# Heads of grouped attention as steps between weight blocks, in a decoder trunk on one core

## The chip, the cores and the metric

One NeuronCore of a Trainium2 chip runs one launch that computes the whole trunk in fp32. The metric is device time in microseconds (us), a median over several runs. TensorE (PE; its weight loads are PEld), VectorE (DVE), ScalarE (ACT), GpSimd (POOL) and SyncE (SP) each work through a queue of their own in order and wait for one another by semaphores.

## The reference

Four layers run over 256 tokens of width 2048. Layers 0 and 3 are latent attention, layer 1 is sparse attention (an indexer picks the keys of each query), layer 2 is sliding-window attention with sinks. Every layer also has four memory heads and a gate:

```
h = rmsnorm(x)
q, k, v, (indexer), mq, gate = split(h @ w_in)
self heads  : softmax(q k^T * scale + bias + mask) v     # 32 heads in 4 groups of 8
memory heads: softmax(mq mk^T * scale) mv                # 4 heads of 256
x = x + ((self ++ memory) * silu(gate)) @ w_out
```

Layers 1 and 2 share one table of relative-position biases, a row for each head. In layer 1 the bias is added to the mask of the selection first; in layer 2 a sink joins the softmax.

## The kernel before, in words

**Weights.** Products keep nearly fp32 precision by being split in two: a value is a high part plus a low part, and three matmuls (high by high, high by low, low by high) make one product. Weights stream from memory once. `stage` issues the load of a block (two tiles of 128x512, 512 KB) on SP's queue into one of five buffers `wr`. `parts_of` turns a tile into `wh` (ScalarE copies it with rounding, L60) and `wl` (VectorE, `wr` minus `wh`, L69); either has three buffers:

```
wh = wp.tile([P, 512], F32R, name="wh", tag="wh", bufs=3)
wl = wp.tile([P, 512], F32R, name="wl", tag="wl", bufs=3)
```

`rows_by` (L265 to L267) multiplies the activations of two blocks of 128 tokens, one PSUM accumulator each, with a block of 512 weight columns, one k tile after the other; `columns_by` (L285, L289) does the same with tokens along the columns, for the gate. PSUM has four accumulators, so two column blocks can be open at a time.

**Parts of a layer.** The branch of a layer has six parts: 4 and 5 are the memory heads in pairs, 0 to 3 the groups of eight self heads. They are taken in the order 4, 0, 1, 2, 3, 5. The output projection `w_out` of a part (four column blocks, four k tiles each, L1139 adds into `x`) is issued one part late: the code for part n+1 goes ahead of that for the projection of part n, which is `pending` until then.

**Grouped attention** (layers 1 and 2, class `Grouped`). `project(g)` multiplies out the queries of group g (`acc_q`), transposes them (`tr`) to `qS`, starts the load of the group's eight bias rows `bm` on POOL's queue and multiplies out the gate (`acc_g`, L483 and L484 its activation). `attend` runs the eight heads in the order 0, 2, 1, 3, 4, 6, 5, 7: scores (`sp`, L943, L946), bias (layer 2: L520, L522; layer 1: L955 first), exponentials (`e`, L527), their transposes (`ptp`, L502), split to `pT` for two heads at a time, and the product with the values (`o`, L972). After heads 1 and 3, and again after 5 and 7, `yt` is `o` times the gate (L978), and is split to the high and low halves of `y` for two of the four k tiles of `w_out`: heads 0 to 3 make k = 0, 1, heads 4 to 7 make k = 2, 3.

**Order.** `steps` is a list of generators: each call of `other_work`, one in every weight block, advances the first of them by two, and what they issue then stands between weight blocks in program order. In the program before they carry other side work (the selection of layer 1 among it), and `attend` issues all eight heads at one place. The order in each engine's queue is then set by the framework's scheduler, which may move an instruction ahead of others as far as dependencies and buffers allow; heads, transposes and weight tiles of neighbouring parts are mixed there already.

Of the kernel before, what the change touches and what calls it, by code (L numbers as in the profile page):

```python
# [8 lines left out]
F32 = mybir.dt.float32  # L9
# [6 lines left out]
P = 128  # L16
S = 256
# [9 lines left out]
N_TAB = 384  # L27
# [4 lines left out]
def kernel(ctx: ExitStack, tc: tile.TileContext, a: dict, out: bass.AP,  # L32
                             kinds=(0, 1, 2, 0)):
    nc = tc.nc
# [18 lines left out]
    def f32(ap):  # L53
        return ap.bitcast(F32)
# [174 lines left out]
    def other_work():  # L229
        for _ in range(2):  # L230
            if steps and next(steps[0], None) is None:
                steps.pop(0)

    def parts_of(wr, c0, n):
        wh = wp.tile([P, 512], F32R, name="wh", tag="wh", bufs=3)
# [238 lines left out]
    def gate(nm, w, c0):  # L474
        gT = act.tile([P, 4, S], F32, name="gT", tag="gT", bufs=2)
        for h in range(2):
            acc = columns_by(nm.at, 16, w, 0, (c0 + h * S, S), "g")
            for j in range(2):
                z = total(acc[j])
                hz = wk.tile([P, S], F32, name="hz", tag="z", bufs=3)  # L480
                nc.vector.tensor_mul(hz, z, nm.half)
                th = wk.tile([P, S], F32, name="th", tag="e", bufs=4)
                nc.scalar.activation(th, hz, AF.Tanh)  # L483
                nc.vector.scalar_tensor_tensor(gT[:, 2 * h + j, :], th, 1.0, hz, op0=OP.add, op1=OP.mult)  # L484
        return gT
# [65 lines left out]
    def memory_project(nm, i, w, mq0, g0, part, behind):  # L551
        kT, qT = [], []
        if part == 0:
            not_before(behind)
        v = [act.tile([P, 2, 512], F32R, name="mvr", tag="aux", bufs=AUX) for z in range(2)]
        pin = tc.keep_in_program_order if part == 0 else lambda inst: inst
        for z in range(2):
            pin(nc.gpsimd.dma_start(v[z], mv[i][part][:, z]))
        for h in range(2):
            k = act.tile([P, 2, 2, S], F32R, name="mkr", tag="pq", bufs=PQ)  # L560
            pin(nc.gpsimd.dma_start(k, mkT[i][2 * part + h]))
            kT.append(k)
            acc = columns_by(nm.at, 16, w, 0, (mq0 + part * 512 + h * 256, 256), "mq")
            q = act.tile([P, 2, 2, S], F32R, name="mqT", tag="pq", bufs=PQ)
            head_parts(q, acc)
            qT.append(q)
        return nm, kT, v, qT, gate(nm, w, g0 + 2048 + part * 512)
# [179 lines left out]
    class Grouped:  # L747
# [165 lines left out]
        def project(self, g):  # L913
            nm = self.nm
            acc = rows_by(nm.at, 16, self.w, 0, (g * 512, 512), "q")
            q = [act.tile([P, 4, S], F32R, name="qS", tag="pq", bufs=PQ) for z in range(2)]
            if self.sparse:
                for z in range(2):
                    rows_ = part_tile(F32)
                    for t in range(2):  # L920
                        copy_act(rows_[:, t * S:(t + 1) * S], acc[t][:, z * S:(z + 1) * S],
                                 scale=nm.col("eighth", t))
                    four_heads(q[z], [rows_[:, t * S:(t + 1) * S] for t in range(2)])
            else:
                for t in range(2):
                    self.stacked(lambda i0, i1: q[i0 // 4][:, :, t * P:(t + 1) * P], acc[t],
                                 nm.col("eighth", t), 8)
            bm = act.tile([P, 8, S], F32, name="bm", tag="big3")
            tab = tabs[0 if self.sparse else 1][g]
            nc.gpsimd.dma_start(bm, bass.AP(tensor=tab.tensor, offset=tab.offset + 127,  # L930
                                            ap=[[8 * N_TAB - 1, P], [N_TAB, 8], [1, S]]))
            return g, q, bm, gate(nm, self.w, self.g0 + g * 512)

        def attend(self, g, q, bm, gT):
            while steps:
                other_work()
            y = act.tile([P, 2, 4, S], F32R, name="y", tag="y", bufs=2)
            for h in (0, 2, 1, 3, 4, 6, 5, 7):
                def score(b):
                    sp = misc("sp")  # L940
                    qb = q[h // 4][:, h % 4, b * P:(b + 1) * P]
                    if b == 0:
                        nc.tensor.matmul(sp[:, :S], qb, self.k[:, g, :, :P], start=True, stop=True)  # L943
                    else:
                        for v in range(2):
                            nc.tensor.matmul(sp[:, :S], qb, self.k[:, g, v, :],  # L946
                                             start=v == 0, stop=v == 1)
                    return sp

                def bias(b, n):  # L950
                    bh = bm[:, h, S - n:]
                    if not self.sparse:
                        return bh
                    bs = wk.tile([P, S], F32, name="bs", tag="e", bufs=4)
                    nc.vector.tensor_add(bs[:, :n], bh, self.sel[:, b, :n])  # L955
                    return bs[:, :n]
                nsk = None if self.sparse else nsink[:, g * 8 + h:g * 8 + h + 1]
                tp = masked_softmax(score, bias, None, nsk)

                half, odd = h // 2 % 2, h % 2  # L960
                if half == 0:
                    pHL = [wk.tile([P, 3, 2, P], F32R, name="pT2", tag="pT", bufs=PT) for z in range(2)]
                split(pHL[0][:, :, half, :], pHL[1][:, :, half, :],
                      tp[:, :3 * P].rearrange("p (i c) -> p i c", i=3))
                if half == 0:
                    continue
                if not odd:
                    o = misc("o")
                v0 = g * P + (0 if odd else 64)
                for t in range(2):  # L970
                    for n_, (z, p_) in enumerate(((0, 0), (0, 1), (1, 0))):
                        nc.tensor.matmul(o[:, t * S:], self.vz[z][:, t, v0:v0 + P],  # L972
                                         pHL[p_][:, 2 * t:2 + t].rearrange("p i h c -> p (i h c)"),
                                         start=odd == t == n_ == 0, stop=odd == t == 1 and n_ == 2)
                if odd:
                    j = (h // 4) * 2
                    yt = tmp("yt")
                    nc.vector.tensor_mul(yt.rearrange("p (j b c) -> p j b c", j=2, b=2),  # L978
                                         o.rearrange("p (b j c) -> p j b c", b=2, j=2),
                                         gT[:, j:j + 2, :].rearrange("p j (b c) -> p j b c", b=2))  # L980
                    split(y[:, 0, j:j + 2, :], y[:, 1, j:j + 2, :], yt.rearrange("p (a b) -> p a b", a=2))
            return y


    def last_out(w, part, y):
# [140 lines left out]
    for i in range(depth):  # L1126
        kind = kinds[i]
        mixer = Latent(nm, i, kinds[:i].count(0)) if kind == 0 else Grouped(nm, i, kind == 1)
        mixer.first()
        if i == depth - 1:  # L1130
            steps.append(split_ahead(a["w_out"][i], 5))
        nxt = Norm(i + 1) if i + 1 < depth else None

        def w_out(part, y, last):
            for c in range(4):
                acc = rows_by([y], 4, a["w_out"][i], part * 4, (c * 512, 512), "wo")
                for t in range(2):
                    xs = x[t][:, c * 512:(c + 1) * 512]
                    nc.vector.tensor_add(xs, xs, acc[t])  # L1139
                if c == 0 and copies:  # L1140

                    not_before(xs[:, :1])
                    table_copies(*copies.pop(0))
                if last and nxt is not None:
                    nxt.chunk(c)

        pending = None
        order = [4, 0, 1, 2, 3, 5]
        for n_, part in enumerate(order):
            if part >= 4:  # L1150
                y = memory_attend(*memory_project(nm, i, mixer.w, mixer.mq0, mixer.g0, part - 4,
                                                  f32(mixer.k[:, 0] if kind else mixer.kr)[:, 0, :1]))
            else:
                y = mixer.attend(*mixer.project(part))
            if pending is not None:
                w_out(*pending, False)
            pending = (part, y)
        if nxt is None:
            last_out(a["w_out"][i], *pending)
        else:  # L1160
            w_out(*pending, True)
            nxt.finish()
            nm = nxt
# [62 lines left out]
```

## Time and profile before

| | us |
|---|---|
| median of 3 runs | 2582.67 |
| lowest and highest | 2582.4, 2584.72 |
| profiled execution | 2583.45 |
| its span, first to last instruction | 2581.7 |
| TensorE busy | 2569.7 (granted clock 0.999) |
| VectorE busy | 1885.5 |
| ScalarE busy | 1618.6 |
| POOL busy | 87.1 |

Busy time is the sum of an engine's instructions with overlaps counted once. Matmuls overlap, so the row of TensorE tells how seldom it stands still, not how fast it is. In the rows below, a line starts with the engine and line of the code (L265 is line 265), the output and its inputs by name, and the shape; `x` is a count, and what stands in brackets or after the last bar is idle time ahead of the instruction and who ended it. In rows by window, each engine has its busy time and its instructions, and then stand the granted clock, the share of the DMA engines and GB/s.

### The profile page before, as it was taken

How to read it: one execution, taken by the hardware profiler on the slowest of the kernel's cores; microseconds unless marked ns; L12 is line 12 of the kernel's file. 1: busy time of each engine (PE TensorE's matmuls, PEld its weight loads, DVE VectorE, ACT ScalarE, POOL GpSimd, SP SyncE). 2: the span in 40 equal slices, each digit the busy share in tenths (PEclk: the TensorE clock that was granted, in tenths of full speed). 3: DMA queues.
4: the chain of work that ended last, by engine and by line, in shares of the span. 5: the costliest groups of instructions: out<-in, count | busy, mean ns of one | idle time of the engine just before them, and what ended most of it. 6: DMA issues, size and time to landing. Idle time of an engine off the chain costs nothing. (4 is left out here: it accounts for less than half of the span.)

```text
span 2581.7 us, 41595 instructions
## 1 busy us (share of the span) xinstructions
PE 2569.7 (100%) x13986; PEld 2210.8 (86%) x13986; DVE 1885.5 (73%) x4139; ACT 1618.6 (63%) x3435; POOL 87.1 (3%) x159
## 2 busy tenths in 40 slices
PE   9999999999999999999999999999999999999998
PEld 7888898888888888888888888888888888888887
DVE  6666667677776686877778776777778767777676
ACT  6556556556656566667666666676666655665655
POOL 1000000000000010000000000000000000000000
PEclk9999999999999999999999999999999999999999
DMA  9888777666676667566556565555555877666664
GB/s 301 257 258 268 239 213 235 183 172 192 192 205 200 199 213 248 169 203 188 190 171 197 171 221 170 173 174 185 196 156 147 241 201 197 196 195 182 211 173 179
DMA packets 459416, 520.02 MB, mean 201 GB/s; under 512 B 69520, under 2 KB 353056, under 8 KB 457536
## 3 DMA queue, kind: packets, MB, share of 16 engines
q1 hardware_dynamic: 441744, 449.72, 58.1%
q0 software_dynamic: 16736, 66.65, 8.0%
q8 instruction: 110, 1.80, 0.3%
q14 instruction: 106, 0.87, 0.1%
q10 hardware_dynamic: 720, 0.98, 0.1%
HBM read 494.10 MB, written 35.75 MB: 205 GB/s over the span
## 5 line engine op out<-in xcount | busy, mean ns | idle before, releaser
L69 DVE TENSOR_TENSOR wl<-wr,wh 128x512 fp32r<-128x512 f32 (+2 forms) x1720 | 1159.9, 677 | 610.0 <-ACT wh L60 588.8
L60 ACT ACTIVATE wh<-wr 128x512 fp32r<-128x512 f32 (+2 forms) x1720 | 1065.3, 621 | 796.6 <-PE acc_g L285 176.9
L285 PE MATMUL acc_g<-xT,wh 128*128 128x512 f32 x1536 | 486.0, 396 | 0.0
L289 PEld LDWEIGHTS acc_g<-xT,wl 128*128 128x128 f32 x1536 | 284.6, 188 | 61.7
L289 PE MATMUL acc_g<-xT,wl 128*128 128x256 f32 x1536 | 307.9, 280 | 0.0
L266 PE MATMUL acc_wo<-wl,y 128*128 128x512 f32 x752 | 297.1, 395 | 0.2 <-DVE wl L69 0.2
L267 PE MATMUL acc_wo<-wh,y 128*128 128x512 f32 x752 | 292.0, 390 | 0.0
L285 PEld LDWEIGHTS acc_g<-xT,wh 128*128 128x128 f32 x1536 | 237.1, 189 | 2.7
L265 PE MATMUL acc_wo<-wh,y 128*128 128x512 f32 x752 | 234.5, 392 | 0.1
L266 PEld LDWEIGHTS acc_wo<-wl,y 128*128 128x128 f32 x752 | 141.3, 188 | 27.9 <-DVE wl L69 0.6
L267 PEld LDWEIGHTS acc_wo<-wh,y 128*128 128x128 f32 x752 | 141.3, 188 | 27.1
L265 PEld LDWEIGHTS acc_wo<-wh,y 128*128 128x128 f32 x752 | 139.1, 188 | 28.7 <-ACT y L60 1.0
L285 PE MATMUL acc_mq<-xT,wh 128*128 128x512 f32 x512 | 161.6, 396 | 0.0
L285 PE MATMUL acc_mk<-mT,wh 128*128 128x512 f32 x512 | 161.5, 396 | 0.1
L1139 DVE TENSOR_TENSOR x<-x,acc_wo 128x512 f32<-128x512 f32 x184 | 121.4, 681 | 3.7 <-PE acc_wo L267 3.6
L285 PE MATMUL acc_qn<-cT,wh 128*128 128x512 f32 x384 | 121.3, 397 | 0.0
L285 PE MATMUL acc_cq<-xT,wh 128*128 128x512 f32 x384 | 120.9, 396 | 0.0
L289 PEld LDWEIGHTS acc_mk<-mT,wl 128*128 128x128 f32 x512 | 96.1, 188 | 22.8 <-DVE wl L69 0.4
L289 PEld LDWEIGHTS acc_mq<-xT,wl 128*128 128x128 f32 x512 | 93.9, 188 | 20.1
L289 PE MATMUL acc_mq<-xT,wl 128*128 128x256 f32 x512 | 103.1, 281 | 0.0
L266 PE MATMUL acc_q<-wl,xT 128*128 128x512 f32 x256 | 101.2, 395 | 0.0
L289 PE MATMUL acc_mk<-mT,wl 128*128 128x256 f32 x512 | 101.1, 278 | 0.0
(328 smaller groups left out, 4326.2 us busy)
## 6 DMA issues: line engine op xcount, KB each, us to landing
wr<-in_w_out_dram SPq DMA_DIRECT2D x188, 512.0 KB, 3.7
wr<-in_w_in_a_dram SPq DMA_DIRECT2D x176, 512.0 KB, 4.5
wr<-in_w_mem_kv_dram SPq DMA_DIRECT2D x120, 512.0 KB, 4.6
wr<-in_w_in_b_dram SPq DMA_DIRECT2D x112, 512.0 KB, 3.4
wr<-in_w_in_c_dram SPq DMA_DIRECT2D x104, 512.0 KB, 3.5
wr<-in_w_uq_dram SPq DMA_DIRECT2D x192, 128.0 KB, 2.9
wr<-in_w_uq_dram SPq DMA_DIRECT2D x48, 256.0 KB, 3.8
tab<-flat POOLq DMA_DIRECT2D x8, 1536.0 KB, 9.7
```

Source lines behind the costliest of these rows:

```text
L60: inst = nc.scalar.activation(o, i, AF.Copy, scale=scale)
L69: nc.vector.tensor_sub(lo, src, f32(hi))
L265: nc.tensor.matmul(acc[t][:, :n], xh, wh[:, :n], start=first, stop=False)
L266: nc.tensor.matmul(acc[t][:, :n], xh, wl[:, :n], start=False, stop=False)
L267: nc.tensor.matmul(acc[t][:, :n], xl, wh[:, :n], start=False, stop=last)
L285: nc.tensor.matmul(acc[j], wh[:, o:o + P], q[:, :, kt % 4, :], start=kt == 0, stop=False)
L289: nc.tensor.matmul(acc[j][:, 0, :], wl[:, o:o + P], q[:, 0, kt % 4, :], start=False, stop=kt == kts - 1)
L1139: nc.vector.tensor_add(xs, xs, acc[t])
```

## The change

The heads of a group become a generator, `heads`, that is appended to `steps`; `attend` only finishes what is in `steps`, loads the second half of the bias rows and allocates `y`. A head is preceded by a count of empty steps (`ahead`), so that heads come one at a time between the weight blocks that follow: the pending output projection (8 blocks), the next group's query projection (8), and its gate (3 of them), with 38 empty steps in all at two in each block. `finish_steps` empties the list: at the next `attend`, and ahead of the memory heads of part 5 in layers 1 and 2. The queries of the next group, and with them their transposes, so stand ahead of the last two heads in program order. The bias rows are one tile for the whole mixer, loaded by halves of four heads: the first after the query projection, the second at `attend`. No arithmetic changes.

```diff
@@ other_work
+    def finish_steps():
+        while steps:
+            other_work()
@@ Grouped.project
-            bm = act.tile([P, 8, S], F32, name="bm", tag="big3")
+            if g == 0:
+                self.bm = act.tile([P, 8, S], F32, name="bm", tag="big3")
+            self.load_bias(g, 0)
+            return g, q, self.bm, gate(nm, self.w, self.g0 + g * 512)
+
+        def load_bias(self, g, half):
             tab = tabs[0 if self.sparse else 1][g]
-            nc.gpsimd.dma_start(bm, bass.AP(tensor=tab.tensor, offset=tab.offset + 127,
-                                            ap=[[8 * N_TAB - 1, P], [N_TAB, 8], [1, S]]))
-            return g, q, bm, gate(nm, self.w, self.g0 + g * 512)
+            nc.gpsimd.dma_start(self.bm[:, 4 * half:4 * half + 4, :],
+                                bass.AP(tensor=tab.tensor, offset=tab.offset + 127 + 4 * half * N_TAB,
+                                        ap=[[8 * N_TAB - 1, P], [N_TAB, 4], [1, S]]))
 
         def attend(self, g, q, bm, gT):
-            while steps:
-                other_work()
+            finish_steps()
+            self.load_bias(g, 1)
             y = act.tile([P, 2, 4, S], F32R, name="y", tag="y", bufs=2)
-            for h in (0, 2, 1, 3, 4, 6, 5, 7):
+            steps.append(self.heads(y, g, q, bm, gT))
+            return y
+
+        def heads(self, y, g, q, bm, gT):
+            for h, ahead in ((0, 0), (2, 6), (1, 6), (3, 5), (4, 4), (6, 4), (5, 5), (7, 7)):
+                for _ in range(ahead):
+                    yield True
                 def score(b):
...
-            return y
@@ the loop over parts
-                y = memory_attend(*memory_project(nm, i, mixer.w, mixer.mq0, mixer.g0, part - 4,
-                                                  f32(mixer.k[:, 0] if kind else mixer.kr)[:, 0, :1]))
+                projected = memory_project(nm, i, mixer.w, mixer.mq0, mixer.g0, part - 4,
+                                           f32(mixer.k[:, 0] if kind else mixer.kr)[:, 0, :1])
+                if kind and part == 5:
+                    finish_steps()
+                y = memory_attend(*projected)
```

## The prediction

> **What bounds the kernel now.** I read the page's busy shares first, then the windows of the stretch that the change touches, then the chain of waits of TensorE (PE) and of its weight loads (PEld), and last the timeline around two hand-overs between groups.
>
> ```profile
> PE 2569.7 (100%) x13986; PEld 2210.8 (86%) x13986; DVE 1885.5 (73%) x4139; ACT 1618.6 (63%) x3435; POOL 87.1 (3%) x159
> ...
> 1100.00:1437.00 337.00, 337.00 (x1798) 287.68 (x1797) 266.84 (x637) 230.35 (x523) 7.38 (x11) 1.00 0.61 190
> 1437.00:1620.00 183.00, 182.54 (x986) 155.65 (x985) 130.80 (x252) 110.69 (x222) 5.43 (x9) 1.00 0.59 186
> 1620.00:1930.00 310.00, 309.66 (x1657) 262.81 (x1655) 238.81 (x602) 212.28 (x520) 3.80 (x5) 1.00 0.57 179
> ...
> PEld acc_wo L265 <- ACT y L60: 1.0, 2, 0.5
> PEld o L972 <- DVE pT L69: 0.8, 1, 0.8
> PEld acc_wo L265 <- ACT wh L60: 0.3, 1, 0.3
> ```
>
> TensorE is the bound, at a granted clock of 1.00. The windows from 1100 to 1620 and to 1930 us hold grouped attention of layers 1 and 2 and what lies between; there TensorE is idle 0, 0.46 and 0.34 us: 0.80 us in 830. The change alters no arithmetic: both programs issue 13,897 matmuls and transposes, 4,125 VectorE and 3,165 ScalarE instructions, and the order on SP's queue is the same. Outside this stretch (the first 6,422 and last 3,347 TensorE instructions) TensorE's order is the same too. So next to nothing is to be won, and the question is whether the new order stays as free of waits as the old one.
>
> **How a weight tile travels, and the distance it needs.** ScalarE copies a 128x512 tile to wh, VectorE makes wl from it, and TensorE reads wh as early as both exist. wh and wl have three buffers each. A copy into a buffer starts when TensorE's last read of the old content has ended:
>
> ```profile
> 1698.53 0.63 PE L267 MATMUL acc_wo<-wh,y 128*128 128x512 f32 x2
> 1699.20 0.63 ACT L60 ACTIVATE wh<-wr 128x512 fp32r<-128x512 f32 x1 [0.20 <-PE acc_wo L267]
> 1699.46 0.39 PE L267 MATMUL acc_wo<-wh,y 128*128 128x512 f32 x1
> 1699.69 0.40 PE L265 MATMUL acc_wo<-wh,y 128*128 128x512 f32 x1
> ...
> 1926.94 0.39 PE L972 MATMUL o<-pT,vz 128*128 128x512 f32 x1
> 1927.67 1.09 PE L972 MATMUL o<-pT,vz 128*128 128x512 f32 x5 [0.34 <-DVE ms L583]
> 1928.80 0.69 DVE L978 TENSOR_TENSOR yt<-o,gT 128x512 f32<-128x512 f32 x1 [0.19 <-PE o L972]
> 1929.53 0.63 ACT L60 ACTIVATE y<-yt 128x512 fp32r<-128x512 f32 x1 [0.62 <-DVE yt L978]
> 1929.74 0.39 PE L267 MATMUL acc_wo<-wh,y 128*128 128x512 f32 x1
> 1930.19 0.69 DVE L69 TENSOR_TENSOR y<-yt,y 128x512 fp32r<-128x512 f32 x1 [0.63 <-ACT y L60]
> 1930.21 0.50 PE L265 MATMUL acc_wo<-wh,y 128*128 128x512 f32 x1
> ```
>
> The pair at 1698.53 ends at 1699.16 and the copy starts 0.04 later. ScalarE's 0.63 at 1929.53 ends at 1930.16 and TensorE starts on its result 0.05 later, VectorE 0.03 later. Matmuls follow each other every 0.23 us though each lasts 0.39. So from the start of the last read to the first use of the next content the chain is 0.39 + 0.04 + 0.63 + 0.05 = **1.11 us**, the time of five matmuls. wl follows wh by 0.03 + 0.69 (VectorE, below) with the same hand-over: 0.72 after wh could first be used. For y, the last o matmul (256 columns, 0.28) is followed by 0.04 + yt 0.69 + 0.04 + y 0.63 + 0.05: **1.73 us** from its start.
>
> **The change, part by part.** (1) Heads become steps, drawn two per weight block, with 38 draws in 19 blocks: eight of the output projection, eight of the next q, three of the gate. The last head falls into the gate's last blocks, right ahead of the output projection that reads its y. (2) The next group's queries are transposed before the last two heads. In the program before, those transposes lay at the hand-over and were what TensorE did while copies were made:
>
> ```profile
> 1689.97 0.88 PE L456 MATMUL tr<-identr,hl 128*128 128x128 f32 x8
> ...
> 1693.73 0.46 PE L456 MATMUL tr<-identr,hl 128*128 128x128 f32 x4
> 1694.02 1.05 PE L972 MATMUL o<-pT,vz 128*128 128x512 f32 x5
> 1694.91 0.46 PE L456 MATMUL tr<-identr,hl 128*128 128x128 f32 x4
> ```
>
> They take the same time wherever they stand; what goes is the cover of 0.88 + 0.46 + 0.46 = 1.8 us. The built program shows what is late next. At a hand-over the output projection's first column block has read its tiles k = 0, 1, and its k = 2, 3 (heads 4 to 7) await y. Their wh are already made and sit in two of the three buffers. TensorE goes on to the second column block, k = 0, 1, whose two wh must pass one after the other through the one buffer left. TensorE's order after, layer 2, from group 0 to 1 (its lines stand 4 lower in the file: L269 is L265, and L506 and L989 are L502 and L972):
>
> ```
> 8672 L270 acc_wo1_19596<-wl_19644
> 8673 L271 acc_wo1_19596<-wh_19643   last read of this buffer
> 8674 L269 acc_wo0_19677<-wh_19681   same buffer, next content
> 8675 L270 acc_wo0_19677<-wl_19682
> 8676 L271 acc_wo0_19677<-wh_19681
> ...  one transpose, three scores
> 8680-8682 acc_wo1_19678<-wh_19681, wl_19682, wh_19681
> 8683 L506 ptp x2
> 8684 L269 acc_wo0_19677<-wh_19691   same buffer again
> 8685 L269 acc_wo1_19678<-wh_19691
> 8686 L270 acc_wo0_19677<-wl_19692
> ...  o, 3 matmuls, o x5, ptp, three scores, ptp x2
> 8700 L269 acc_wo0_19595<-wh_19655   needs the last y
> ```
>
> The durations for the walk (VectorE, ScalarE, in the window of layer 2; the last rows are SP's, and POOL's):
>
> ```profile
> L69 DVE TENSOR_TENSOR wl<-wr,wh 128x512 fp32r<-128x512 f32 x193 | 132.6, 689 | 53.9 <-ACT wh L60 50.4 <-PE acc_g L285 1.9 <-PE acc_mq L285 0.7
> L60 ACT ACTIVATE wh<-wr 128x512 fp32r<-128x512 f32 x192 | 120.7, 630 | 77.8 <-PE acc_g L285 19.5 <-PE acc_wo L267 18.4 <-DVE mn L522 16.8
> L60 ACT ACTIVATE pT<-ptp 128x384 fp32r<-128x384 f32 x32 | 15.5, 484 | 6.7 <-PE ptp L502 6.4
> L483 ACT ACTIVATE th<-hz 128x256 f32<-128x256 f32 x16 | 6.5, 408 | 0.3 <-DVE hz L481 0.3
> L481 DVE TENSOR_TENSOR hz<-z,half 128x256 f32<-128x256 f32 x16 | 6.7, 419 | 0.2
> L520 DVE TENSOR_TENSOR u<-sp,bm 128x128 f32<-128x128 f32 x32 | 9.2, 286 | 9.2 <-PE sp L943 9.2
> L972 PE MATMUL o<-pT,vz 128*128 128x256 f32 x48 | 8.3, 281 | 0.0
> wr<-in_w_out_dram SPq DMA_DIRECT2D x188, 512.0 KB, 3.7
> 1836.45 0.88 POOL L930 DMA_DIRECT2D bm<-tab  x1 [76.50 <-DVE mn L522]
> 1837.32 1.13 POOL L561 DMA_DIRECT2D mkr<-mkT  x2
> ```
>
> *A hand-over in layer 2.* wh_19681 has one matmul of distance: 1.11 − 0.23 = 0.88, and ScalarE has a th of the gate queued ahead of it (0.41, of which 0.27 falls behind the release): 1.15. wl_19682 has one matmul: 0.72 − 0.23 = 0.49, and VectorE an hz (0.42) of which 0.2 is left: 0.7. wh_19691 has the two transposes as well (0.45 in all): 0.66. wl_19692 has two matmuls: 0.27. The last y has the o matmul, three transposes and three scores ahead of it, seven at 0.11 (an estimate: they have 128 or 256 columns, and 512 take 0.23), 0.78 of its 1.73: 0.95, and the copy of y stands behind a pT copy (0.48, 0.28 of it in the way): 1.23. Sum 1.15 + 0.7 + 0.66 + 0.27 + 1.23 = 4.0; with both engines free, 3.25. It stands at two of the three hand-overs (0 to 1 and 2 to 3); at 1 to 2 the distances hold.
>
> *A hand-over in layer 1* (all three). The o matmuls stand between wh and wl there, and y comes in time; the wh distances are 0.46 and 0.23: 0.65 + 0.88 = 1.53.
>
> *The ends of the layers.* At the end of layer 1 a head's pT has some 0.27 less distance than its chain needs; I take 0.3. At the end of layer 2 heads are done early in the new order (its last o is 9.6 us of matmuls ahead of the y use), and the waits shown above go: 1926.94 + 0.23 to 1927.67 is 0.50, 1929.74 + 0.23 to 1930.21 is 0.24. The 0.3 on wh in the rows of waits goes with the order: 1.0 removed.
>
> *The rest costs nothing.* While TensorE stands, everything behind it in its queue is late by the same amount, once. SP's loads: five buffers of two tiles, each 12 matmuls of 0.23 = 2.8 us, cover 14 us against a landing of 3.7. (3) The bias halves add 8 issues of 0.9 us on POOL, at 3% busy; behind them stand only loads of mkr, which memory attention reads 90 us later. The first half needs only heads 0 to 3 of the group before to be done, the second is issued some 25 draws (12 blocks) ahead of head 4. If that cover were gone, a landing of 7.5 us would stand before u:
>
> ```profile
> L930 POOL DMA_DIRECT2D bm<-tab x8: 882/907/921, 1014.8 to 1836.4; - x8
> ...
> DMA to landing us min/median/max: 6.1/7.5/9.7
> ```
>
> u waits only for scores in the row of L520 above (9.2 of 9.2 us), so halves gain nothing. The Trainium skill says otherwise (Perfetto Trace Analysis, DMA Optimizations): splitting transfers can let some work start sooner, where DMA engines are idle. By that rule the change would win at most the stretch's 0.80 us of idle TensorE; the trace does not bear it out, as u never waits for bm.
>
> *Sum.* 3 × 1.53 + 2 × 4.0 + 0.3 − 1.0 = 4.6 + 8.0 + 0.3 − 1.0 = **+11.9 us**. The profiled execution took 2583.45 us (span 2581.7, 1.75 around it), so 2595.35 on its own time; it lies 0.78 above the median of 2582.67, on which the forecast is **2594.6**. With ScalarE and VectorE always free at the release: 4.6 + 6.5 − 1.0 = +10.1, 2592.8. If half of the waits are hidden: +5.5, 2588.2. If ScalarE's and VectorE's queues delay each of the 16 waits of the hand-overs by another 0.25: +15.9, 2598.6.
>
> **Rivals.** *Not slower.* The program before parks tiles at the hand-over as well and loses only the 0.3 us on wh. If five matmuls still lie between last read and next use on the chip, only the 1.0 us of removed waits is left: 2581.7. It decides at a distance of 1.11 us. For it: the old order's rows. Against it: one matmul, 0.23 us, in the built order. 0.09. *No change, since the bound's work is unchanged*: TensorE is 100% busy and gets the same instructions; 2582.7. For it: 0.80 us idle in 830. Against it: an order can add waits to a busy engine, as the y waits of 1.0 in the rows show. 0.04. The Trainium skill would see it so (Perfetto Trace Analysis, Identifying Performance Opportunities): improving a kernel generally means improving its most-contended engine, found by occupancy. *Half hidden*, because copies are released earlier than at a read's modelled end: 2588.2, 0.12. *Longer queues*, above: 2598.6, 0.14. *The change doesn't do what it says*: the built order shows that it does.
>
> **How the numbers follow.** The forecast, 2594.6, has 0.61; the other chances stand with their rivals. The range, 2588 to 2598.6, holds the forecast, half of the half-hidden case and most of the longer queues: about 0.8. About 0.2% (5.2 us) is what a measurement can tell from no change, so slower begins at 2587.8: forecast, longer queues and two thirds of the half-hidden case, 0.83. The rest of that case, no change and not slower make same 0.15, and 0.02 is left for faster, which would take more than all waits of the stretch.
>
> **What would show it.** In the profile after, the waits of TensorE and PEld should list acc_wo on ScalarE's wh for 6 to 9 us over ten places, on VectorE's wl for some 2 and on y for 2 to 3; the window of layer 1's groups should be longer by some 5 us, that of layer 2 by some 7, and the rest alike. No such rows, or waits of u on bm, would prove the steps wrong.

## The result, and the profile after

| | before | after |
|---|---|---|
| median, us | 2582.64 | 2599.24 |
| lowest and highest of 6 | 2582.4, 2584.72 | 2598.07, 2601.51 |
| profiled execution, span | 2583.45, 2581.7 | 2598.07, 2596.3 |

The change is slower by 16.6 us, a ratio of 1.0064 (95% interval 1.0051 to 1.0077). The direction was forecast and the size was not: +11.9 was forecast, and the median lies 0.6 above the range's upper end. In the profiles the spans differ by 14.6, but the starts of the program differ as well. Counted by the starts of the same TensorE instructions, the groups of layer 1 (the 6,400th to the 7,950th instruction) take 289.0 us before and 295.9 after, +6.9, and those of layer 2 (the 9,050th to the 10,640th) 296.4 and 305.4, +9.0.

The windows of the stretch that the change reorders, in the profile after (columns as before). They cover the same clock times and so slightly less work than before, but TensorE's idle time can be read off: 3.66, 0.18 and 6.26 us, against 0, 0.46 and 0.34.

```profile
1100.00:1437.00 337.00, 333.34 (x1758) 281.17 (x1757) 263.50 (x622) 224.88 (x507) 8.01 (x13) 1.00 0.60 186
1437.00:1620.00 183.00, 182.82 (x994) 155.77 (x993) 131.03 (x257) 111.99 (x228) 6.89 (x11) 1.00 0.60 187
1620.00:1930.00 310.00, 303.74 (x1602) 255.72 (x1601) 233.09 (x587) 207.89 (x509) 5.64 (x8) 0.99 0.56 173
```

The waits of TensorE and of its weight loads after; the numbers are us in total, times, and the longest:

```profile
PE acc_wo L269 <- ACT wh L60: 6.8, 10, 1.1
PE acc_wo L269 <- ACT y L60: 2.2, 2, 1.1
...
PE acc_wo L270 <- DVE wl L69: 0.9, 2, 0.4
...
PEld acc_wo L269 <- ACT wh L60: 10.7, 11, 1.6
PEld acc_wo L270 <- DVE wl L69: 2.7, 5, 0.8
...
PEld acc_g L293 <- DVE wl L69: 1.2, 3, 0.4
```

They stand where the built order had them: ten waits on wh, five hand-overs with two each, and two on the last y. The slow hand-over of layer 2, from group 0 to 1, on TensorE, and after it the rows of ScalarE around the first wait:

```profile
1699.39 0.39 PE L271 MATMUL acc_wo<-wh,y 128*128 128x512 f32 x1
1700.92 0.50 PE L269 MATMUL acc_wo<-wh,y 128*128 128x512 f32 x1 [1.14 <-ACT wh L60]
1701.86 0.50 PE L270 MATMUL acc_wo<-wl,y 128*128 128x512 f32 x1 [0.44 <-DVE wl L69]
1702.20 0.39 PE L271 MATMUL acc_wo<-wh,y 128*128 128x512 f32 x1
...
1704.54 0.73 PE L269 MATMUL acc_wo<-wh,y 128*128 128x512 f32 x2 [0.56 <-ACT wh L60]
1705.26 0.50 PE L270 MATMUL acc_wo<-wl,y 128*128 128x512 f32 x1
...
1709.30 0.50 PE L269 MATMUL acc_wo<-wh,y 128*128 128x512 f32 x1 [1.10 <-ACT y L60]
1709.64 0.39 PE L270 MATMUL acc_wo<-wl,y 128*128 128x512 f32 x1
1709.87 0.39 PE L269 MATMUL acc_wo<-wh,y 128*128 128x512 f32 x1
...
1699.54 0.40 ACT L487 ACTIVATE th<-hz 128x256 f32<-128x256 f32 x1
1699.94 0.40 ACT L487 ACTIVATE th<-hz 128x256 f32<-128x256 f32 x1
1700.25 0.61 ACT L60 ACTIVATE wh<-wr 128x512 fp32r<-128x512 f32 x1
```

Read from start to start: 1699.39 to 1700.92 is 1.53, of which 0.23 is the matmul, so the wait costs 1.30. The last read of the buffer ended at 1699.78, and the copy started at 1700.25, behind the second th. The next wait (wl) costs 1.86 − 0.92 − 0.23 = 0.71. The wait for y is the largest single one, about 1.34: the "1.10" in brackets counts from the modelled end of the matmul ahead, not from where the next could have started.

A hand-over of layer 1, where two waits on wh stand:

```profile
1210.80 0.43 PE L989 MATMUL o<-pT,vz 128*128 128x512 f32 x1
1211.73 0.73 PE L269 MATMUL acc_wo<-wh,y 128*128 128x512 f32 x2 [0.50 <-ACT wh L60]
...
1213.82 0.39 PE L271 MATMUL acc_wo<-wh,y 128*128 128x512 f32 x1
1214.93 1.02 PE L269 MATMUL acc_wo<-wh,y 128*128 128x512 f32 x3 [0.72 <-ACT wh L60]
```

1211.73 − 1210.80 − 0.23 = 0.70 and 1214.93 − 1213.82 − 0.23 = 0.88, where the forecast had 0.65 and 0.88.

At the other slow hand-over of layer 2, from group 2 to 3, something else is added. The windows there (the number behind POOL's count is the granted clock), and two matmuls:

```profile
1862.00:1864.00 2.00, 2.00 (x8) 1.60 (x8) 1.18 (x5) 0.42 (x1) 0.00 (x0) 0.50 1.05 378
1864.00:1866.00 2.00, 1.65 (x7) 0.86 (x6) 1.51 (x5) 1.88 (x7) 0.00 (x0) 0.66 0.10 36
...
1862.54 0.63 PE L269 MATMUL acc_wo<-wh,y 128*128 128x512 f32 x1
1862.97 0.63 PE L270 MATMUL acc_wo<-wl,y 128*128 128x512 f32 x1
```

The clock falls to a half for some 3.4 us (2 us at 0.50, and 2 us of which the mean is 0.66, so another 1.4), and matmuls follow each other every 0.43 us in place of 0.23.

### The profile page after: what moved, and what is told of

Same layout as the page of the kernel before. It is cut to its first block, busy times and chain, and to the rows that moved or that the text cites. A ratio compares the mean times of both kernels' runs of the same rounds, so it can differ in the third digit from the quotient of the medians.

```text
span 2596.3 us, 41621 instructions
## 1 busy us (share of the span) xinstructions
PE 2575.6 (99%) x13986; PEld 2210.4 (85%) x13986; DVE 1888.7 (73%) x4139; ACT 1619.6 (62%) x3435; POOL 91.7 (4%) x167
## 5 line engine op out<-in xcount | busy, mean ns | idle before, releaser
L293 PEld LDWEIGHTS acc_g<-xT,wl 128*128 128x128 f32 x1536 | 284.5, 188 | 63.3 <-DVE wl L69 1.2
L293 PE MATMUL acc_g<-xT,wl 128*128 128x256 f32 x1536 | 306.6, 280 | 0.0
L269 PEld LDWEIGHTS acc_wo<-wh,y 128*128 128x128 f32 x752 | 138.0, 188 | 40.3 <-ACT wh L60 10.7
L293 PEld LDWEIGHTS acc_mk<-mT,wl 128*128 128x128 f32 x512 | 96.1, 188 | 22.8 <-DVE wl L69 0.4
L293 PEld LDWEIGHTS acc_mq<-xT,wl 128*128 128x128 f32 x512 | 94.1, 188 | 20.4
L293 PE MATMUL acc_mq<-xT,wl 128*128 128x256 f32 x512 | 102.9, 281 | 0.0
L293 PE MATMUL acc_mk<-mT,wl 128*128 128x256 f32 x512 | 101.1, 278 | 0.0
```

Source lines behind the costliest of these rows:

```text
L269: nc.tensor.matmul(acc[t][:, :n], xh, wh[:, :n], start=first, stop=False)
L293: nc.tensor.matmul(acc[j][:, 0, :], wl[:, o:o + P], q[:, 0, kt % 4, :], start=False, stop=kt == kts - 1)
```

## The experiments

**Is it the place of the last heads, or steps and halves as such?** The heads stay steps, with fewer empty ones:

```diff
-            for h, ahead in ((0, 0), (2, 6), (1, 6), (3, 5), (4, 4), (6, 4), (5, 5), (7, 7)):
+            for h, ahead in ((0, 0), (2, 5), (1, 4), (3, 4), (4, 4), (6, 4), (5, 4), (7, 5)):
```

> The change with other counts of empty steps (5, 4, 4, 4, 4, 4, 5: 30 in all, against 38): heads are still steps between weight blocks and the bias rows still come by halves, but all eight heads stand ahead of the next queries' transposes in program order. Theory A (the last heads behind those transposes make y late, which parks two wh tiles): the hand-overs are as before, no waits on wh over 0.3 us, 2582.6 us. Theory B (steps and bias halves themselves mix ScalarE's and VectorE's queues, or POOL's loads, so that copies are late): 2596 to 2599.

Measured: 2582.55 against 2582.97 on the same chip, ratio 0.9999 (0.999 to 1.0008). The built order of TensorE, ScalarE, VectorE and SP is that of the program before, instruction by instruction, though the code issues the heads one by one over 16 blocks; only POOL's queue has the halves. So 30 empty steps change nothing in the order that is built, and the larger counts of the change do. Those add up to 37 empty steps, not 38, and to 38 draws: head 5 comes with draw 31, head 7 with draw 38, and the next group's queries are multiplied out by draw 32. By this count the last head alone, not the last two, stands behind the next group's transposes. Theory B falls: the bias halves and the steps as such cost nothing. The waits of TensorE, in full but for the first microseconds of the span:

```profile
PE o L989 <- DVE pT L69: 0.3, 1, 0.3
PE acc_wo L270 <- DVE wl L69: 0.2, 1, 0.2
```

**The two layers apart**, by issuing the heads in one place unless

```diff
-            steps.append(self.heads(y, g, q, bm, gT))
+            hs = self.heads(y, g, q, bm, gT)
+            if self.sparse:          # layer 1 alone; "not self.sparse" for layer 2 alone
+                steps.append(hs)
+            else:
+                for _ in hs:
+                    pass
```

> Heads as steps in layer 1 alone; in layer 2 they are issued in one place as before, with bias halves kept. Theory A: the three hand-overs of layer 1 cost what the profile after shows there, 2.2 us each (waits of 0.68 and 0.88 on wh, and 0.1 of restart for each of some five stalled matmuls), and the end of layer 1 0.6: 6.6 + 0.6 = 7.2, so 2589.8, with executions within 0.5 us of each other, since these waits leave the granted clock at 1.00. If the excess over the forecast lay in longer queues in layer 2 alone, layer 1 would be worth only the forecast's 4.6 + 0.3: 2587.5.

> Heads as steps in layer 2 alone. Theory A with a clock that falls to a half for about 3 us after such a stretch of waits in some executions: 4.6 us at each of two hand-overs, 1.8 removed at the end of layer 2 and ahead of it: 2582.6 + 7.4 = 2590.0 without a fall of the clock, 1.5 more for each one, so executions spread from 2590 to 2593. Without the clock (all of the excess in queues): executions within 0.5 us of each other. Layer 1 alone and layer 2 alone should add up to the change's +16.6 within 1.

> The changed kernel itself, for a second profile and more executions. Theory A with the clock: the same waits to 0.05 us at the same places, but falls of the granted clock at other places or in another number; spans are longer by about 1.5 us for each one. If the spread of executions (2598.1 to 2601.5) is in the waits, the rows of waits will differ.

Measured, against 2582.97: layer 1 alone 2589.40 (2588.95 to 2590.21; ratio 1.0026, 1.0016 to 1.0035), layer 2 alone 2592.56 (2590.65 to 2594.45; 1.0036, 1.0024 to 1.0049), the change again 2598.81 (2597.45 to 2599.15; 1.0059, 1.0046 to 1.0072). So 6.4 + 9.6 = 16.0 against 15.8: the parts add up. Layer 1 costs 6.4, not the forecast's 4.9, with the same two waits at each hand-over, so queues in layer 2 are not the only excess. Two of the expectations on spread missed: layer 1 alone, which has no fall of the clock in its profile, spread over 1.3 us and not 0.5, and layer 2 alone reached 2594.45 and not 2593. In the second profile of the change the waits stand at the same places with the same lengths, and the granted clock is 1.00 throughout that stretch. Layer 1 costs 6.9 there too, and layer 2 costs 8.0 in place of 9.0. Its span is 2596.1, with a wait of 0.6 on the load of mkr that the first did not have.

**How much does a fall of the clock cost?** Layer 2 alone, three more executions:

> Layer 2 alone once more, for a profile of another execution. Theory with the clock: the waits are those of the earlier profile to 0.05 us, and the execution is near 2590.7, 2592.6 or 2594.5 with no, one or two stretches of granted clock 0.50 at the hand-overs. Without the clock: times differ with no such stretch, by other waits.

> As the look before: the number of stretches at a granted clock of 0.50 goes with the time, 1.9 us each at most.

> As the two looks before: the number of stretches at a granted clock of 0.50 goes with the time, 1.9 us each at most.

The times were 2594.83, 2592.68 and 2592.90, and that of the first profile 2590.70. The falls, in windows of the first look and of the third:

```profile
1698.00:1700.00 2.00, 2.00 (x7) 1.61 (x8) 1.35 (x7) 0.67 (x2) 0.00 (x0) 0.50 0.66 244
```

```profile
1698.00:1700.00 2.00, 1.71 (x5) 1.13 (x4) 1.74 (x7) 1.58 (x5) 0.00 (x0) 0.50 0.00 0
1856.00:1858.00 2.00, 2.00 (x10) 1.53 (x11) 1.79 (x7) 1.07 (x4) 0.00 (x0) 0.78 1.10 394
1858.00:1860.00 2.00, 1.71 (x6) 1.07 (x5) 1.83 (x7) 1.85 (x8) 0.00 (x0) 0.50 0.35 132
```

The number of falls at hand-overs is 0, 1, 1 and 2 for 2590.70, 2594.83, 2592.68 and 2592.90: the falls are real, but the expectation of 1.9 us each, and of times in steps of it, fell. Timed over a hand-over, from the last matmul ahead of the first wait to the second matmul after the wait for y, the first takes 10.47 us without a fall and 11.56, 11.17 and 11.19 with one; the second takes 10.80 to 10.82 without and 11.47 with one. In the change it is 10.25 without and 11.24 with. A fall costs 0.7 to 1.1, since part of the slow stretch lies in the next wait, which is shorter then. The rest of the spread is elsewhere: in the execution at 2594.83 the first loads of the program came late, the clock fell to a half once more at 11.8 to 15.2 us, and a wait of 0.4 on mkr stood ahead of layer 2. TensorE's 61st matmul starts at 16.6, 19.0, 17.8 and 17.2 us in the four profiles, so up to 2.4 us of the difference lies in the start. Such differences are in every kernel's runs: those of the program before spread over 2.0 us in that series.

**When does the clock fall?** The traces' records of the granted clock tell more than these windows. In all fourteen profiles of this case every change of the clock lies a whole number of steps of 3.413 us behind the first record, and a fall lasts one step or two. The first step starts at another place in every execution (3.9 to 9.8 us into the span), so the steps cut the same waits differently. Below are, of the profile after, the step ahead of the fall and the fall; then, of the second look at layer 2, the same two steps of the first slow hand-over, and the step with the first waits of the second one:

```profile
1858.55:1861.96 3.41, 1.83 (x8) 0.95 (x7) 3.29 (x10) 3.12 (x10) 0.79 (x2) 1.00 0.74 219
1861.96:1865.37 3.41, 3.06 (x11) 2.19 (x10) 2.11 (x8) 1.67 (x5) 0.00 (x0) 0.50 0.68 246
```

```profile
1693.80:1697.21 3.41, 1.83 (x10) 1.28 (x10) 3.26 (x11) 2.85 (x9) 0.00 (x0) 1.00 0.87 280
1697.21:1700.62 3.41, 3.12 (x9) 2.13 (x8) 2.83 (x11) 2.44 (x9) 0.00 (x0) 0.50 0.07 28
...
1854.23:1857.64 3.41, 1.87 (x9) 1.38 (x10) 3.22 (x12) 2.85 (x9) 0.12 (x1) 1.00 0.96 302
```

TensorE is busy for 1.83 us of the step ahead of each of these falls; the step with 1.87 us has none behind it. It is so in all fourteen profiles while TensorE works: the twelve falls from the full clock each follow a step with 1.84 us or less, and no step with 1.87 us or more was followed by one. So it is where the steps happen to cut the waits that decides whether a slow hand-over has a fall, and with the same program that changes from one execution to the next.

**One hand-over alone** (the condition `not self.sparse and g == 0` in the diff above):

> Heads as steps for the first group of layer 2 alone, so one hand-over of the slow kind is left. Theory A with the clock: 4.6 to 5.2 more than before, 2587.6, in two clusters of executions, the upper one up to 1.9 above the lower (a clock at a half for some 3.3 us loses about 1.7, less where it falls into a wait). Without the clock: one cluster, about 1 us wide.

Measured: 2587.35 against 2582.94 (2586.72 to 2589.05; ratio 1.0019, 1.001 to 1.0028), +4.4, 0.2 less than the least that was expected. Neither two clusters nor one of 1 us can be told in the eleven times, and its profile has no fall, so this run says nothing on the clock.

```profile
PE acc_wo L269 <- ACT wh L60: 1.9, 2, 1.1
PE acc_wo L269 <- ACT y L60: 1.4, 1, 1.4
```

**Is the late y the cause?** The output projection takes its k tiles 2 and 3 from the first half of y, heads 0 to 3, in every part of every layer, so that what heads 4 to 7 made is left out:

```diff
+                kk = (s + k) % 2 if name == "wo" else (s + k) % 4
...
-                    xh, xl = (q[:, v, (s + k) % 4, t * P:(t + 1) * P] for v in range(2))
+                    xh, xl = (q[:, v, kk, t * P:(t + 1) * P] for v in range(2))
```

> The changed kernel, but the output projection multiplies its k tiles 2 and 3 by y of heads 0 to 3 in place of heads 4 to 7 (as many matmuls of the same shapes), so that no tile awaits the last heads. Theory A (the late y parks two wh tiles): with no tile parked, the waits on wh, wl and y at the hand-overs are gone, those of the program before too: 2580.5 to 2582. Theory B (ScalarE and VectorE are too busy there, whoever waits): the wh waits stay, 2593 or more, and only the y waits of 2.7 go.

Measured: 2582.05 against 2582.94, ratio 0.9998 (0.9988 to 1.0007): all 16 us are gone. What is left in the rows of TensorE's waits, in full, is the span's first microseconds:

```profile
PE wu L102 <- DVE ones L98: 1.1, 1, 1.1
PE acc_mv L270 <- ACT wh L60: 0.5, 2, 0.3
```

ScalarE and VectorE have the same work in this kernel as in the change. Theory A holds: they are not too slow, but were handed the wrong tiles first. The three short waits of weight loads on wl in layer 1's gate (acc_g, 1.2 us in all) are still there, so those don't come of the late y. The scheduler builds another order when that dependence goes, so this shows that the late y is at the root and not which of its effects costs most.

**Is it the parked tiles?** Column blocks by pairs, in all layers, so that the copies for k = 2, 3 come later in program order (`ST` is 2):

```diff
+    def rows_pair(y, w, k0, blocks):
...
+        for s in range(0, 4, ST):
+            for c, acc in zip(blocks, accs):
+                wr, n = stage(w, k0 + s, ST, (c * 512, 512))
...
             for c in range(4):
-                acc = rows_by([y], 4, a["w_out"][i], part * 4, (c * 512, 512), "wo")
+                if c not in accs:
+                    group = [p for p in [(0, 1), (2, 3)] if c in p] or [(c,)]
+                    accs.update(zip(group[0], rows_pair(y, a["w_out"][i], part * 4, group[0])))
+                acc = accs[c]
```

> The changed kernel, with the output projection's column blocks taken in pairs: k = 0, 1 of both blocks first in program order, then k = 2, 3 of both, so that the copies of k = 2, 3 come behind those that TensorE can use. y is as late as in the change. Theory A: the wh waits of layer 1 (1.56 and restarts, 2.2 a hand-over) nearly go; the last y is still late in layer 2, 1 to 4 us a hand-over: 2586 to 2591. If parked tiles aren't the cause: 2597 to 2600.

Measured: 2592.92 against 2582.94 (ratio 1.004, 1.0025 to 1.0054), 5.9 below the change's median in the other series and 1.9 above what was expected. Its waits in grouped attention:

```profile
PE acc_wo L285 <- ACT y L60: 3.0, 5, 1.4
PE ptp L522 <- ACT e L60: 1.2, 2, 0.8
...
PE o L1005 <- ACT pT L60: 1.1, 1, 1.1
...
PE o L1005 <- DVE pT L69: 0.6, 1, 0.6
```

Of the output projection's waits on wh none is left in TensorE's own rows, and 0.9 us in those of its weight loads, where there were 10.7. So parked tiles were what made those. By TensorE's instructions counted as above, layer 1 costs about 2 us in place of 6.9, and layer 2 about 9 as before. There TensorE now waits for y itself and for the heads that make it; this profile also has a fall of the clock, of two steps, at 1859 to 1865 us. That TensorE has nothing else to read meanwhile is argued, not shown.

**Would a fourth buffer help?**

```diff
-        wh = wp.tile([P, 512], F32R, name="wh", tag="wh", bufs=3)
+        wh = wp.tile([P, 512], F32R, name="wh", tag="wh", bufs=4)
-        return wk.tile([P, n], dt, name=name, tag=f"t{n}", bufs=3)
+        return wk.tile([P, n], dt, name=name, tag=f"t{n}", bufs=2)
```

> The changed kernel with a fourth buffer for wh (its room from a ring of temporaries, three to two). Theory A in its plain form (one buffer is left, so a fourth adds one): the wh waits of 6.8 us and their restarts go, 2589 to 2592. Rival C: the scheduler orders copies as far ahead as buffers let it, so a fourth is filled with one more copy that isn't needed yet, ahead of heads' work on ScalarE and VectorE, and the waits move to their results: 2598 to 2612.

Measured: 2616.87 against 2582.94, ratio 1.0133 (1.0118 to 1.0147): 18 us slower than the change. The wait on wh in the output projection is 0.7, and others take its place:

```profile
PE ptp L506 <- ACT e L60: 6.9, 3, 3.4
PE acc_wo L269 <- ACT y L60: 5.1, 7, 1.1
PE acc_wo L269 <- DVE z L300: 4.5, 3, 2.2
PE acc_wo L270 <- DVE wl L69: 2.3, 5, 0.8
```

That is rival C's outcome and not theory A's plain form. It also goes against a reading that the Trainium skill suggests (Perfetto Trace Analysis, Optimization Strategy): that the same gap coming back on the busiest engine can mean too few buffers for the next tile. The wh wait was such a gap; with the fourth buffer, and the smaller ring of temporaries, it went, and the kernel was 18 us slower. That the fourth buffer is filled ahead of the heads' work is argued from where the waits went; a fourth buffer within the same order was not tried, as the scheduler makes a new order for it, and the ring of temporaries is smaller here as well. All five hand-overs have a fall of the clock in this profile, one of them:

```profile
1716.00:1718.00 2.00, 0.22 (x1) 0.00 (x0) 1.39 (x6) 1.50 (x7) 0.67 (x1) 0.92 0.89 275
1718.00:1720.00 2.00, 1.67 (x4) 1.39 (x5) 1.39 (x4) 1.30 (x4) 0.00 (x0) 0.50 0.66 231
```

**A version that might beat both**: the program before, with the pairs above for blocks 0 and 1 of the self parts of layers 1 and 2 alone.

> The program before (heads in one place, whole bias rows), with the first two column blocks of the output projection taken as a pair for the self parts of layers 1 and 2 alone: k = 0, 1 of both, then k = 2, 3 of both. Theory A: the waits of the program before at hand-overs and at the ends of layers 1 and 2 on y, wh and wl (some 1.5 us with their restarts) go and another of 0.9 comes at the end of layer 2: 2582, 0.5 to 1.5 us under the program before, at the edge of what can be told. If the pairing cost something of its own: 2584 or more.

Measured: 2581.98 against 2582.86, ratio 0.9996 (0.9987 to 1.0005). It lies where expected, and can't be told from no change. In its profile TensorE's waits on y, wh and wl in grouped attention are gone, and one of 0.7 on a pT of memory attention is there instead.

## Why the prediction was right in kind and wrong in size

*Bound and places.* Right: next to nothing was to be won, and the waits came at five hand-overs, two on wh each, with wl and y in layer 2. The late y is the root of the waits at the hand-overs, as the run without that dependence shows, and parked tiles make the wh waits, as the pairs show. The rivals "not slower" and "no change" fell: the distance of one matmul was as short on the chip as in the built order.

*A hand-over of layer 1: 1.53 forecast.* The waits of 0.70 and 0.88 are as walked. **The step that failed is the price of a wait**: the walk stopped at the awaited tile and put what follows at nothing. After a wait TensorE needs 0.34 from the stalled matmul to the next in place of 0.23 (1709.30 to 1709.64, then 1709.87). That restart of 0.11 stood in the rows of before that the prediction quotes: at 1930.21 the stalled matmul lasts 0.50, not 0.39. It follows each of the 16 waits of the hand-overs, 1.7 us in all, and is the largest term that was missing. Layer 1 alone cost 6.4 by the medians, and 6.9 by TensorE's instructions, where 3 × 1.53 + 0.3 = 4.9 was forecast. Of the 1.5 to 2 between, two restarts at three hand-overs are 0.7; the walk also overlooked a short wait on wl in the gate ahead of each hand-over (the row acc_g L293, three times), 0.14 from start to start and a restart behind it, 0.25 each and 0.75 in all. The end of layer 1 cost 0.4, near the 0.3 that was taken.

*A hand-over of layer 2: 4.0 forecast.* Walked against measured: first wh 1.15 and 1.30 (two th stood ahead, where 0.27 was taken), wl 0.7 and 0.71, second wh 0.66 and about 0.8, second wl 0.27 and 0.15, last y 1.23 and about 1.3. The restarts come to five times 0.11, 0.55. So a hand-over has 4.8 us of waits and restarts where 4.0 was taken. Without a fall of the clock layer 2 cost 8.0 in the change where 8.0 − 1.0 = 7.0 was forecast; that is 0.6 less than these waits add up to, and where the 0.6 was won stays open.

*The clock.* The forecast took the granted clock at 1.00, as every window before had it. It falls to 0.50 in some executions at hand-overs of layer 2, at a price of 0.7 to 1.1 each, and the profile after holds one. It is the second missing term: a term of chance, which the range should have held. Layers 1 and 2 without a fall cost 6.9 + 8.0, 14.9 in place of 11.9; one fall adds 1.0. The "longer queues" rival had nearly the right size, 2598.6, by luck: a wait was not longer by 0.25 in the queues, but by less than 0.1 on average, and had a restart of 0.11 behind it.

*The parts that cost nothing* were right: bias halves and steps (2582.55 with both), SP's loads. The waits removed at the end of layer 2 are gone, too: TensorE's two waits on y are those of the hand-overs, and its wait of o on VectorE is not among the rows after.

*From the profile to the median.* The forecast was to be 0.78 below the profiled execution, and the median is 1.17 above it. Over the change's eleven executions times run from 2597.45 to 2601.51. A fall of the clock moves an execution by about a microsecond, and the start by more: TensorE's 61st matmul starts at 16.3 to 19.0 us in the fourteen profiles. How many falls the slowest executions had stays open, since there is no trace of them.

## What to carry to other kernels

Where a scheduler orders by readiness, what counts in a reordering is which tile ends up waiting, and which buffers the copies made for it hold meanwhile: count the matmuls between a buffer's last read and its next use, against the chain that refills it. Price a wait by the awaited tile, the restart behind it, and the fall of the clock that a cluster of waits may bring. One more buffer is no remedy by itself, as it changes the order too.

## What the runs showed of the hardware

A stalled 512-column matmul is followed by the next after 0.34 us, not 0.23. Two waits of 1.30 and 0.71 us, with one matmul between, were followed by a granted clock of 0.50 for about 3.4 us in some executions and not in others, with the same waits at the same places: four of the eight slow hand-overs of the four profiles of layer 2 alone had one. All changes of the clock in the fourteen profiles lie on steps of 3.413 us; a step in which TensorE was busy for 1.84 us or less was followed by a fall, and from the full clock one with 1.87 us or more was not. The Trainium skill (TensorE: Matmul & The Clock Gate, What's actually happening) puts the half clock behind at least one idle window of about 3.4 us. The length of the slow stretch agrees with such a window; but TensorE was busy for 1.83 us of the step ahead of the fall, so the window need not be idle throughout.
